# The upper column half of gates and projections with tokens stationary and 512 weight columns moving

## The chip, the cores and the metric

The kernel runs on one core of one Trainium2 chip. A time is device microseconds of one execution. The kernel before took 1406.93 us (median of three runs, 1406.03 to 1407.38). One execution was profiled; it took 1405.17 us, and its trace spans 1403.3 us.

## The reference

One block of a decoder, 256 tokens of width 2048, float32. In short:

```python
mod = silu(c) @ w_ada + b_ada                 # six vectors of 2048: sh1, sc1, g1, sh2, sc2, g2
h = rms_norm(x, norm_mix_g) * (1 + sc1) + sh1
u, q, k, v, ga, gb = split(h @ w_in)          # 1024 each, the two gates 2048 each
y_ssm = s5_branch(u, ...)                     # a scan over tokens, gelu, then y * sigmoid(y @ w_glu + b_glu)
y_att = moba_attention(q, k, v, rel_bias)     # 8 heads of 128, causal, with a bias by distance
merged = sigmoid(ga) * (y_ssm @ w_proj_ssm) + sigmoid(gb) * (y_att @ w_proj_attn)
x = x + g1 * (merged @ w_out)
h2 = rms_norm(x, norm_mlp_g) * (1 + sc2) + sh2
x = x + g2 * (square(relu(h2 @ w_ff1)) @ w_ff2)
return rms_norm(x, norm_final_g)
```

With 256 tokens there is one attention block, so attention is plain causal attention with a bias.

## The kernel before

**Arithmetic.** Every large product is made of three TensorE products in a shorter float format. Each operand is split into a high part, a copy by ScalarE (`split`, L144), and a low part, the difference, by VectorE (L146). A GEMM adds high x high, high x low and low x high in one PSUM bank.

**Weights.** All weights are streamed in tiles of 128 rows by 1024 columns (512 KB; `load`, L139, on SP's queue) into seven buffers `wraw`. ScalarE makes `whi`, VectorE `wlo`, with four buffers each, so the splits can be at most four steps ahead of TensorE. A *step* below is one such tile: its splits and its matmuls.

**Two forms of a GEMM.** In `gemm_t` (L172, matmuls L188 to L190) a 128x128 piece of the weights is stationary and the 256 tokens move; the result has output columns on the partitions. A step has 8 x 3 = 24 matmuls. In `gemm_n` (L297, L315 to L319) 128 tokens are stationary and 512 weight columns move; the result has tokens on the partitions. A step has 2 x 2 x 3 = 12 matmuls. Both fill four PSUM banks for 1024 columns; five banks are there for them (`bank`), three for the smaller work (`aux`), so of four banks of a new GEMM only the first is free before the last GEMM's banks are emptied.

**Stages.** Each stage of the table further down is a run of such GEMMs. First come eight column blocks of w_in (q, k, v, u and the lower half of gate ga) in parts, as the first modulation vectors become ready (`qkvu`). Then, with all 16 steps each: ga upper, gb lower, gb upper (the loop at L1138, i = 1, 2, 3). Then the projections with 8 steps each: `proj_attn(0)`, the GLU, `proj_attn(1)`, and the two halves of the SSM projection (L1187). Then w_out, the norm, and the MLP.

**What runs beside it.** *Lanes* are lists of small jobs; after each step every lane gains its rate and issues a job for each whole unit (`step`). The lane "ada" holds the products with w_ada that are not needed at once: each job loads 512 KB into a `wraw` buffer and VectorE multiplies and sums it (L374, 1.22 us). Its rate is set by stage: R2 and R3 in `qkvu`, RS0 to RS2 in the gates, RPA from the projections on, RWO in w_out. The lane "m" holds attention, head by head (scores `sco`, softmax on VectorE and ScalarE, transposes `ptr`, values `pav`), and from the middle of ga upper on the SSM branch in four parts (`ssm_in`: `vr` and `vi` on TensorE; `ssm_scan` on VectorE; `ssm_ys`: `ys`), then gelu and the way back to channel order.

**Order.** Within each engine instructions run in the order in which they stand. A scheduler sets that order when the program is built; it works from its own estimate of the times and from priorities (weight loads and splits stand ahead of their place in the code by `OFF`).

**Buffers that matter here.** Attention's scratch `asc` is six of the eight upper slices of ga (`ga[:, 8:14]`, L1110), two heads in turn. The gate's own result is copied there from PSUM by ScalarE (L1144) when attention has let go of the slices. `merged` is split into `mh` and `ml` in the buffer that held `ah` and `al`.

**Token order.** The SSM branch works on tokens in four interleaved phases (token = 4c + s). Before the change the GLU and the SSM projection keep the order (s, c), and the product with the gate reads and writes ga in permuted order (L1192).

Of the kernel before, what the change touches and what calls it, by code (L numbers as in the profile page):

```python
# [15 lines left out]
AF = mybir.ActivationFunctionType  # L16
# [3 lines left out]
P = 128  # L20
S = 256
# [25 lines left out]
SL = 6  # L47
R1 = 1.65
R2 = .95
R3 = .5  # L50
RS0 = .7
RS1 = .25
RS2 = .7
GR = (4, 6, 6)
RAT = 1.5
RSS = .43
RPA = .75
RWO = .5
RM = .55
NP = 4  # L60
# [13 lines left out]
class Kern:  # L74
# [219 lines left out]
            then.append((o, c))  # L294
        yield then

    def gemm_n(self, src, kts, c0, xh, xl, koff=0, tail=1, seeds=None):  # L297
        nc = self.nc
        banks = self.seeded("pn", seeds)
        n = len(kts)  # L300
        held, prev = [], None
        for i, unit in enumerate(self.stream(src, kts, c0)):
            u = (i,) + unit
            held.append(u)
            for t in range(2):
                if t and n - tail <= i < n - 1:
                    continue
                tk = slice(t * P, (t + 1) * P)
                for s in range(2):
                    o = banks[t * 2 + s]  # L310
                    c = slice(s * 512, (s + 1) * 512)
                    for q, kt, hi, lo in held if t else [u]:
                        kx = kt - koff
                        with self.after(prev if tail > 1 and i == n - 1 and t + s else None):
                            nc.tensor.matmul(o, xh[:, kx, tk], hi[:, c], start=q == 0 and not seeds, stop=False,  # L315
                                             skip_group_check=bool(seeds))
                            nc.tensor.matmul(o, xl[:, kx, tk], hi[:, c], start=False, stop=False,  # L317
                                             skip_group_check=bool(seeds))
                            self.mm = last = nc.tensor.matmul(o, xh[:, kx, tk], lo[:, c], start=False, stop=q == n - 1,  # L319
                                                              skip_group_check=bool(seeds))  # L320
                    prev = last
                if t:
                    held = []
        return banks
# [595 lines left out]
    def body(self):  # L920
# [217 lines left out]
        for i in range(1, 4):  # L1138
            if i == 3:
                self.lanes["ada"][1] = RS2  # L1140
            dst, c0 = ((ga, 4096), (ga, 5120), (gb, 6144), (gb, 7168))[i]
            banks = self.gemm_t(win, range(KT), c0, self.ah, self.al, mid=to_ssm if i == 1 else None)
            for b in range(4):
                nc.scalar.copy(dst[:, (i % 2) * 8 + 2 * b:(i % 2) * 8 + 2 * b + 2, :],  # L1144
                               banks[b].rearrange("p (k s) -> p k s", s=S))
# [11 lines left out]
        for k in range(4):  # L1157
            self.split(yh[:, 2 * k:2 * k + 2], yl[:, 2 * k:2 * k + 2], self.yatt[:, 2 * k:2 * k + 2])
        def proj_attn(cg):
            banks = self.gemm_t(a["w_proj_attn"][0], range(8), cg * 1024, yh, yl)  # L1160
            for b in range(4):
                d = gb[:, cg * 8 + 2 * b:cg * 8 + 2 * b + 2, :].rearrange("p k s -> p (k s)")
                v.tensor_mul(d, d, banks[b])
# [12 lines left out]
        for b in range(4):  # L1176
            t = sg[:, b]
            for k in range(2):
                nc.scalar.activation(t[:, k], banks[b][:, k * S:(k + 1) * S], AF.Sigmoid,
                                     bias=self.bglu[:, 2 * b + k:2 * b + k + 1])  # L1180
            s = slice(2 * b, 2 * b + 2)
            v.tensor_mul(sc4(t), sc4(t), yT[:, s])
            self.split(gg[:, 0, s], gg[:, 1, s], t)
        proj_attn(1)
        self.a2("mh")
        mh, ml = self.ah, self.al
        for cg in range(2):  # L1187
            banks = self.gemm_t(a["w_proj_ssm"][0], range(8), cg * 1024, gg[:, 0], gg[:, 1])
            for b in range(4):
                s = slice(cg * 8 + 2 * b, cg * 8 + 2 * b + 2)  # L1190
                d = ga[:, s, :]
                dk = d.rearrange("p k (c s) -> p k s c", s=4)  # L1192
                v.tensor_mul(dk, dk, banks[b].rearrange("p (k s c) -> p k s c", k=2, s=4))
                v.tensor_add(d, d, gb[:, s, :])
                self.split(mh[:, s], ml[:, s], d)
        self.lane("x", self.load_x(), .25, -.5)
        self.lane("g1", [lambda ch=ch: g1_row(ch) for ch in range(4)], .25)
        self.lanes["ada"][1] = RWO
# [261 lines left out]
```

## Time and profile before

| what | value |
|---|---|
| median of the runs | 1406.93 us |
| profiled execution | 1405.17 us, span 1403.3 us |
| TensorE busy | 98% of the span |
| VectorE busy | 74% |
| ScalarE busy | 53% |
| mean granted TensorE clock | 0.996 |

The stages that the prediction speaks of, in us from the span's start, by the first matmul of each:

| stage | form | steps | from | to |
|---|---|---|---|---|
| last third of the w_in blocks | both | 42 | 176.7 | 300.4 |
| ga upper | tokens moving | 16 | 300.4 | 360.6 |
| gb lower | tokens moving | 16 | 360.6 | 417.3 |
| gb upper | tokens moving | 16 | 417.3 | 471.9 |
| attention projection, first half; GLU | tokens moving | 8 + 8 | 471.9 | 518.4 |
| attention projection, second half | tokens moving | 8 | 518.4 | 541.5 |
| SSM projection, two halves | tokens moving | 8 + 8 | 541.5 | 589.7 |
| w_out, first half | weights moving | 16 | 589.7 | 634.4 |

A row of the view by stretches gives the stretch, its length, and for each engine the busy time and (x) the number of instructions, then the granted TensorE clock, the DMA engines' mean busy share and GB/s. A row of the view by groups gives source line, engine, operation, tiles (out<-in), shape and count, then busy time and mean ns of one, then the engine's idle time ahead of them and what ended it. A row of the timeline, or of the chain of waits, begins with start and length. PE is TensorE's matmuls, PEld its weight loads, DVE is VectorE, ACT is ScalarE. A matmul's recorded length includes its way through the array, so matmuls that follow each other overlap and their rate is read from their starts.

### The profile page before, as it was taken

To read this page: it belongs to the slowest core of one execution; us is meant where nothing else is said; L and a number is where in the kernel's file an instruction comes from. 1 tells how busy PE (TensorE), PEld (TensorE's weight loads), DVE (VectorE), ACT (ScalarE), POOL (GpSimd) and SP (SyncE) were. 2 spreads that over 40 slices of the span, in tenths; PEclk is the share of its full clock that TensorE was granted. 3 is DMA by queue.
4 is the path that set the end of the run, shared out by engine and by line. 5 is a ranking of instruction groups with operands and counts; after the bars stand their busy time and mean duration, and the time that the engine had idled before them with its cause. 6 is when DMAs were issued, how large, how long until landed. Compare 5 with 4: busy or idle time off the path is not lost.

```text
span 1403.3 us, 23470 instructions
## 1 busy us (share of the span) xinstructions
PE 1369.2 (98%) x9282; PEld 1219.2 (87%) x9282; DVE 1040.4 (74%) x1474; ACT 737.7 (53%) x1004; POOL 40.9 (3%) x94
## 2 busy tenths in 40 slices
PE   7889999999999999999999999999999999999997
PEld 5779899989999999988888888888888888888885
DVE  5788899776898888977777775777676555554676
ACT  4464565577545853446555554544463553635543
POOL 1000000410001300000000000000000000000000
PEclk9999999999999999999999999999999999999998
DMA  9999996885567988887588777778777566565551
GB/s 352 361 395 332 336 324 221 231 272 205 175 212 236 314 325 301 301 332 291 175 300 282 216 244 246 242 251 276 250 249 235 192 195 190 186 194 187 181 204 60
DMA packets 113293, 353.19 MB, mean 252 GB/s; under 512 B 12080, under 2 KB 12096, under 8 KB 113056
## 3 DMA queue, kind: packets, MB, share of 16 engines
q1 hardware_dynamic: 110096, 346.61, 72.1%
q0 software_dynamic: 2800, 4.58, 1.3%
q8 instruction: 72, 1.18, 0.3%
q10 hardware_dynamic: 288, 0.52, 0.1%
q14 instruction: 37, 0.30, 0.1%
HBM read 347.27 MB, written 2.29 MB: 249 GB/s over the span
## 4 chain that ended last, share of the span: by engine, by line
PE 86%; DMA 7%; DVE 4%; ACT 2%; issue 1%; DVEq 0%; SPq 0%; ACTq 0%
PE pw L216 15%; PE pn L315 9%; PE pn L317 9%; PE pn L319 9%; PE pt L188 8%; PE pt L190 8%; PE pt L189 8%; PE pw L218 8%; DMA wraw<-in_w_in_dram 5%; DVE wlo L146 2%; PE pn L246 2%; PE pn L247 2%; PE pn L248 2%; DVE wraw L374 1%; ACT whi L144 1%
## 5 line engine op out<-in xcount | busy, mean ns | idle before, releaser
L146 DVE TENSOR_TENSOR wlo<-wraw,whi 128x1024 fp32r<-128x1024 f32 x439 | 535.8, 1223 | 276.6 <-ACT whi L144 275.3
L144 ACT CAST whi<-wraw 128x1024 fp32r<-128x1024 f32 x439 | 460.5, 1051 | 531.7 <-PE pn L317 167.8
L216 PE MATMUL pw<-mh,whi 128*128 128x512 f32 x896 | 314.5, 397 | 0.0
L188 PE MATMUL pt<-ah,whi 128*128 128x256 f32 x896 | 251.9, 288 | 5.9 <-ACT whi L144 3.8
L189 PE MATMUL pt<-ah,whi 128*128 128x256 f32 x896 | 249.5, 284 | 0.0
L218 PE MATMUL pw<-mh,wlo 128*128 128x256 f32 x896 | 249.2, 281 | 0.0
L190 PE MATMUL pt<-ah,wlo 128*128 128x256 f32 x896 | 239.7, 286 | 1.4 <-DVE wlo L146 1.1
L374 DVE SCALAR_TENSOR_TENSOR wraw<-wraw,cb 128x1024 f32<-128x1024 f32 x176 | 213.5, 1219 | 0.0
L216 PEld LDWEIGHTS pw<-mh,whi 128*128 128x128 f32 x896 | 167.9, 188 | 39.5
L317 PE MATMUL pn<-whi,ff 128*128 128x512 f32 x480 | 187.0, 390 | 0.0
L315 PE MATMUL pn<-whi,ff 128*128 128x512 f32 x480 | 186.9, 389 | 0.0
L319 PE MATMUL pn<-wlo,ff 128*128 128x512 f32 x480 | 185.8, 389 | 0.0
L188 PEld LDWEIGHTS pt<-ah,whi 128*128 128x128 f32 x896 | 171.6, 192 | 10.3 <-ACT whi L144 5.4
L189 PEld LDWEIGHTS pt<-ah,whi 128*128 128x128 f32 x896 | 172.1, 192 | 0.4 <-DVE ah L146 0.2
L218 PEld LDWEIGHTS pw<-mh,wlo 128*128 128x128 f32 x896 | 169.1, 189 | 1.0
L190 PEld LDWEIGHTS pt<-ah,wlo 128*128 128x128 f32 x896 | 165.0, 192 | 3.8 <-DVE wlo L146 3.4
L315 PEld LDWEIGHTS pn<-whi,ff 128*128 128x128 f32 x480 | 90.1, 188 | 19.0
L319 PEld LDWEIGHTS pn<-wlo,ff 128*128 128x128 f32 x480 | 90.1, 188 | 18.7
L317 PEld LDWEIGHTS pn<-whi,ff 128*128 128x128 f32 x480 | 90.1, 188 | 18.5
L1354 DVE TENSOR_TENSOR y<-y,pn 128x512 f32<-128x512 f32 x48 | 31.0, 684 | 14.6 <-PE pn L319 14.6
L315 PE MATMUL pn<-whi,mh 128*128 128x512 f32 x96 | 37.7, 393 | 1.7 <-ACT whi L144 1.7
L317 PE MATMUL pn<-whi,mh 128*128 128x512 f32 x96 | 37.4, 389 | 0.0
(422 smaller groups left out, 1737.4 us busy)
## 6 DMA issues: line engine op xcount, KB each, us to landing
wraw<-in_w_ff_dram SPq DMA_DIRECT2D x256, 512.0 KB, 4.3
wraw<-in_wat_dram SPq DMA_DIRECT2D x176, 512.0 KB, 5.7
wraw<-in_w_in_dram SPq DMA_DIRECT2D x128, 512.0 KB, 5.5
wraw<-in_w_out_dram SPq DMA_DIRECT2D x32, 512.0 KB, 6.3
wraw<-in_wan_dram SPq DMA_DIRECT2D x16, 512.0 KB, 8.7
wraw<-in_w_proj_attn_dram SPq DMA_DIRECT2D x16, 512.0 KB, 6.5
wraw<-in_w_proj_ssm_dram SPq DMA_DIRECT2D x16, 512.0 KB, 6.7
wraw<-in_w_glu_dram SPq DMA_DIRECT2D x8, 512.0 KB, 5.7
```

Source lines behind the costliest of these rows:

```text
L144: h = self.nc.scalar.copy(hi, src)
L146: s = self.nc.vector.tensor_sub(lo, src, hi.bitcast(F32))
L188: nc.tensor.matmul(o, hi[:, c], xh[:, kx, :], start=st, stop=False, skip_group_check=True)
L189: nc.tensor.matmul(o, hi[:, c], xl[:, kx, :], start=False, stop=False, skip_group_check=True)
L190: self.mm = nc.tensor.matmul(o, lo[:, c], xh[:, kx, :], start=False, stop=sp, skip_group_check=True)
L216: nc.tensor.matmul(banks[b], hi[:, c], x2[:, k0 + k].rearrange("p h s -> p (h s)"), start=i + k == 0, stop=False, skip_group_check=True)
L218: self.mm = nc.tensor.matmul(banks[b][:, 0:S], lo[:, c], x2[:, k0 + k, 0, :], start=False, stop=i == n - 1 and k == 1, skip_group_check=True)
L315: nc.tensor.matmul(o, xh[:, kx, tk], hi[:, c], start=q == 0 and not seeds, stop=False, skip_group_check=bool(seeds))
L317: nc.tensor.matmul(o, xl[:, kx, tk], hi[:, c], start=False, stop=False, skip_group_check=bool(seeds))
L319: self.mm = last = nc.tensor.matmul(o, xh[:, kx, tk], lo[:, c], start=False, stop=q == n - 1, skip_group_check=bool(seeds))
L374: v.scalar_tensor_tensor(w, w, 1.0, self.cb[:, (i % 2) * 1024:(i % 2 + 1) * 1024], op0=OP.mult, op1=OP.mult, accum_out=pc[:, i:i + 1])
L1354: v.tensor_add(d, d, banks[b])
```

## The change

The upper 1024 columns of both gates, of the attention projection and of the SSM projection are computed by `gemm_n` instead of `gemm_t`: 16 + 16 + 8 + 8 steps. Their results, the gate products and the sum then have tokens on the partitions. The merged rows of that half are brought back by 16 transposes on TensorE (four for each PSUM bank) and split from PSUM. The GLU's sigmoid writes its result in natural token order, and what follows (its product with y, the SSM projection, the merge) uses that order, so that the product with ga is no longer permuted. `gemm_n` gets a call-back in its middle, which ga upper needs. The rate of the ada lane goes from .5 to .8 in the last part of `qkvu` (R3) and from .75 to .55 in the projections (RPA).

```diff
-R3 = .5
+R3 = .8
...
-RPA = .75
+RPA = .55
...
-    def gemm_n(self, src, kts, c0, xh, xl, koff=0, tail=1, seeds=None):
+    def gemm_n(self, src, kts, c0, xh, xl, koff=0, tail=1, seeds=None, mid=None):
...
+            if mid and i == n // 2:
+                mid()
...
-            banks = self.gemm_t(win, range(KT), c0, self.ah, self.al, mid=to_ssm if i == 1 else None)
+            gemm = self.gemm_n if i % 2 else self.gemm_t
+            banks = gemm(win, range(KT), c0, self.ah, self.al, mid=to_ssm if i == 1 else None)
...
-            banks = self.gemm_t(a["w_proj_attn"][0], range(8), cg * 1024, yh, yl)
+            banks = (self.gemm_n if cg else self.gemm_t)(a["w_proj_attn"][0], range(8), cg * 1024, yh, yl)
...
-                nc.scalar.activation(t[:, k], banks[b][:, k * S:(k + 1) * S], AF.Sigmoid,
+                nc.scalar.activation(t[:, k].rearrange("p (c s) -> p s c", s=4),
+                                     banks[b][:, k * S:(k + 1) * S].rearrange("p (s c) -> p s c", s=4), AF.Sigmoid,
                                      bias=self.bglu[:, 2 * b + k:2 * b + k + 1])
             s = slice(2 * b, 2 * b + 2)
-            v.tensor_mul(sc4(t), sc4(t), yT[:, s])
+            v.tensor_mul(t.rearrange("p k (c s) -> p k c s", s=4), t.rearrange("p k (c s) -> p k c s", s=4),
+                         self.yT.rearrange("p s k c -> p k c s")[:, s])
...
-            banks = self.gemm_t(a["w_proj_ssm"][0], range(8), cg * 1024, gg[:, 0], gg[:, 1])
+            banks = (self.gemm_n if cg else self.gemm_t)(a["w_proj_ssm"][0], range(8), cg * 1024, gg[:, 0], gg[:, 1])
...
-                dk = d.rearrange("p k (c s) -> p k s c", s=4)
-                v.tensor_mul(dk, dk, banks[b].rearrange("p (k s c) -> p k s c", k=2, s=4))
+                v.tensor_mul(d, d, banks[b].rearrange("p (k s) -> p k s", k=2))
                 v.tensor_add(d, d, gb[:, s, :])
-                self.split(mh[:, s], ml[:, s], d)
+                if cg == 0:
+                    self.split(mh[:, s], ml[:, s], d)
+                    continue
+                p = self.aux("trm")
+                flat = d.rearrange("p k s -> p (k s)")
+                for k in range(4):
+                    nc.tensor.transpose(p[:, k * P:(k + 1) * P], flat[:, k * P:(k + 1) * P], self.ident)
+                ks, tk = slice(8 + 4 * (b % 2), 12 + 4 * (b % 2)), slice(b // 2 * P, (b // 2 + 1) * P)
+                self.split(mh[:, ks, tk], ml[:, ks, tk], p.rearrange("p (k s) -> p k s", s=P))
```

The scheduler lays the work out anew. Three places matter. (In the change all lines stand two or three further down.)

On TensorE, the end of ga upper. Before, the last head's value product and the first SSM input block stand within the last step of ga upper (`pt_3426` to `pt_3429` are its banks):

```order
L188 MATMUL pt_3427<-ah,whi 128x256
L781 MATMUL pav<-ga,v 128x256
L782 MATMUL pav<-ga,v 128x128
L864 MATMUL vr<-u_3045,bp 64x64 x16
L864 MATMUL vi<-u_3045,bp 64x64 x16
L189 MATMUL pt_3427<-ah,whi 128x256
```

Now, in gb lower (`pt_4012` to `pt_4015`), where the third bank is first used:

```order
L188 MATMUL pt_4013<-ah,whi 128x256
L189 MATMUL pt_4013<-ah,whi 128x256
L190 MATMUL pt_4013<-ah,wlo 128x256
L783 MATMUL pav<-ga,v 128x256
L784 MATMUL pav<-ga,v 128x128
L775 MATMUL ptr<-ident,ga 128x128 x3
L188 MATMUL pt_4014<-ah,whi 128x256
L189 MATMUL pt_4014<-ah,whi 128x256
```

This value product is the seventh head's and the transposes are the eighth's. The value products of three heads (the sixth to the eighth) and the first SSM input block have moved from ga upper into the first steps of gb lower, and the first two banks of gb lower go through four steps before its third begins.

On VectorE, the late steps of gb lower, where the splits of the weights and the SSM scans alternate. Now, between the splits of steps 14 and 15 (`rw`, `sri`, `tbl` are the SSM branch's tiles; sixteen such operations stand here, these are the first and the last):

```order
L146 TENSOR_TENSOR wlo<-wraw,whi 128x1024
L873 TENSOR_TENSOR rw<-rw 128x512
L874 TENSOR_TENSOR rw<-vi,tbl 128x512
L883 SCALAR_TENSOR_TENSOR rw<-rw 128x512
...
L892 TENSOR_TENSOR sri<-sri,rw 128x8x63
L871 TENSOR_TENSOR rw<-vr,tbl 128x512
L872 TENSOR_TENSOR rw<-vi,tbl 128x512
L146 TENSOR_TENSOR wlo<-wraw,whi 128x1024
```

Before, the longest such block in this stage is eight operations. The SSM branch's second part starts later and catches up here.

On TensorE, the first half of w_out. Now, 41 matmuls after its start (`pn_6475` to `pn_6478` are its banks):

```order
L321 MATMUL pn_6477<-wlo,mh 128x512
L317 MATMUL pn_6478<-whi,mh 128x512
L319 MATMUL pn_6478<-whi,mh 128x512
L321 MATMUL pn_6478<-wlo,mh 128x512
L321 MATMUL pn_6475<-wlo,mh 128x512
L1205 MATMUL trm<-ident,ga 128x128 x12
L321 MATMUL pn_6476<-wlo,mh 128x512
```

Twelve of the sixteen new transposes stand there together, the other four some three steps later; before, there is nothing but matmuls of w_out and a few small transposes for g1 in this place.

## The prediction

> **What bounds the kernel now.** I read the page first, then the busy times by stage, then single instructions in order of time.
>
> ```profile
> span 1403.3 us, 23470 instructions
> PE 1369.2 (98%) x9282; PEld 1219.2 (87%) x9282; DVE 1040.4 (74%) x1474; ACT 737.7 (53%) x1004; POOL 40.9 (3%) x94
> PE 86%; DMA 7%; DVE 4%; ACT 2%; issue 1%; DVEq 0%; SPq 0%; ACTq 0%
> ```
>
> TensorE is busy for 98% of the span and holds 86% of the chain of waits. An average hides stages, so the next view cuts the stretch that is edited. In order: the last third of the first GEMM phase; gates ga upper, gb lower, gb upper; attention projection (first half) with the GLU; its second half; the two halves of the SSM projection; the first half of w_out.
>
> ```profile
> core 0: us, PE busy (x) PEld busy (x) DVE busy (x) ACT busy (x) POOL busy (x), PEclk, DMA share, GB/s
> 176.70:300.40 123.70, 123.38 (x1317) 117.91 (x1317) 105.33 (x144) 74.17 (x112) 19.67 (x40) 1.00 0.79 254
> 300.40:360.60 60.20, 60.19 (x526) 58.79 (x525) 41.24 (x75) 41.28 (x82) 0.00 (x0) 1.00 0.67 235
> 360.60:417.30 56.70, 56.70 (x707) 55.90 (x705) 54.95 (x72) 28.78 (x35) 0.00 (x0) 1.00 0.57 183
> 417.30:471.90 54.60, 54.60 (x642) 54.00 (x641) 47.21 (x68) 31.38 (x39) 15.26 (x32) 1.00 0.77 253
> 471.90:518.40 46.50, 46.50 (x390) 46.50 (x389) 38.69 (x53) 27.64 (x34) 0.07 (x1) 1.00 0.90 324
> 518.40:541.50 23.10, 23.10 (x195) 23.10 (x194) 20.86 (x32) 12.24 (x18) 0.00 (x0) 1.00 0.91 315
> 541.50:564.50 23.00, 23.00 (x194) 23.00 (x194) 19.13 (x25) 8.39 (x8) 0.00 (x0) 1.00 0.90 327
> 564.50:589.70 25.20, 23.50 (x194) 23.21 (x193) 24.40 (x33) 10.38 (x12) 0.00 (x0) 1.00 0.78 269
> 589.70:634.40 44.70, 44.70 (x206) 37.09 (x205) 37.34 (x48) 20.65 (x23) 0.00 (x0) 1.00 0.89 342
> ```
>
> Everywhere but in the last SSM projection (1.7 us of TensorE idle) PE equals the window, at clock 1.00. So what shortens the PE queue in these stages shortens the span, as long as VectorE keeps up: it stands at 97% in the gb lower gate and in the last SSM projection.
>
> **The main term: matmul pitch.** A busy PE is not a PE at its peak, so I take the starts. First a stretch with weights stationary and 256 tokens moving, then one of the first w_out half, with tokens stationary and 512 columns moving:
>
> ```profile
> 544.82 0.28 PE L189 MATMUL pt<-gg,whi 128*128 128x256 f32 x1
> ...
> 546.25 0.28 PE L190 MATMUL pt<-gg,wlo 128*128 128x256 f32 x1
> ```
> ```profile
> 619.68 0.39 PE L317 MATMUL pn<-whi,mh 128*128 128x512 f32 x1
> ...
> 622.18 0.39 PE L315 MATMUL pn<-whi,mh 128*128 128x512 f32 x1
> ```
>
> The first pair lies 12 matmuls apart: 1.43/12 = 0.119 us. The SSM projection's first half agrees: 8 steps of 24 matmuls in 23.00 us are 0.120. The second pair lies 11 apart: 2.50/11 = 0.227 us. A step over 128 rows of the weights costs 24 x 0.120 = 2.88 us the old way and 12 x 0.227 = 2.72 us the new way. The four edited GEMMs have 16 + 16 + 8 + 8 = 48 steps, so this is 48 x 0.156 = **-7.5 us** (by 0.119 it would be -6.4, by the exact 23.00/192 and 2.50/11 -7.1; with 0.226 -8.1: -6.4 to -8.1).
>
> In the Trainium skill, "TensorE: Matmul & The Clock Gate", section "Back-to-back issue gap", a warm matmul alone costs N/2.4 + 2.5 ns: 109 and 216 ns. By it, as an estimate, two narrow matmuls against a wide one save 2.5 ns, 1.4 us over the 576 pairs. The trace does not agree: 2 x 0.120 - 0.227 leaves 13 ns a pair.
>
> **Transposes of the merged rows.** 16 new TensorE transposes, 128x128, are the same operation as these:
>
> ```profile
> 820.99 1.47 PE L1296 MATMUL trf<-ident,part 128*128 128x128 f32 x12
> L1296 PE MATMUL trf<-ident,part 128*128 128x128 f32 x16 | 2.1, 272 | 0.0
> ```
>
> (1.47 - 0.27)/11 = 0.109 us each, so 16 x 0.109 = **+1.75 us**. They stand on PE within w_out, where PE is the bound: nothing hides them. They are issued 41 matmuls (9.3 us) after w_out begins, and VectorE's four products and four sums before them need 8 x 0.69 = 5.5 us, so they should not be waited for. The upper half of the merged rows is first needed at step 8, 21.8 us in.
>
> **VectorE in the projections.** Two rows of the stretch from the ga upper gate to w_out, the product read in permuted order and the one read straight, then the two standing costs of a step, from the page:
>
> ```profile
> L1193 DVE TENSOR_TENSOR ga<-ga,pt 128x512 f32<-128x512 f32 x8 | 8.7, 1106 | 0.0
> L1163 DVE TENSOR_TENSOR gb<-gb,pt 128x512 f32<-128x512 f32 x8 | 5.1, 681 | 0.0
> ```
> ```profile
> L146 DVE TENSOR_TENSOR wlo<-wraw,whi 128x1024 fp32r<-128x1024 f32 x439 | 535.8, 1223 | 276.6 <-ACT whi L144 275.3
> L374 DVE SCALAR_TENSOR_TENSOR wraw<-wraw,cb 128x1024 f32<-128x1024 f32 x176 | 213.5, 1219 | 0.0
> ```
>
> Eight products go from 1.106 to 0.68 us (-3.4 us of VectorE), and the lower w_ada rate takes 8 sums of 1.22 us out of the projections (30 to 22 in VectorE's queue). The GLU's four products and eight sigmoids now stride; were they all 1.1 us it would be +1.7 on VectorE, behind the 21.8 us of the projection that follows. So VectorE has 103.1 - 3.4 - 9.8 + 1.7 = 91.6 us of work in the four projection windows, of 115.3, instead of 103.1 of 117.8. Does that remove the one stall?
>
> ```profile
> 577.09 6.31 DMA wraw<-in_w_out_dram
> 583.50 1.05 ACT whi L144
> 584.60 0.50 PE pn L315
> ```
>
> The first w_out tile is asked for at 577.1, when VectorE at last frees a buffer, and PE waits for its ScalarE copy until 584.6. The window's 25.2 us less 8 x 2.88 are 2.2, of which two early w_out matmuls take 0.2. All 2.0 may go (-2.0); or VectorE's block of sums and splits after the first SSM half stays as late and PE only arrives 8 x 0.156 = 1.25 us earlier (+1.25). In the new order that block is undivided (eight operations, 5.5 us) but with one w_ada sum ahead of it instead of several. I take half of the gain: **-1.0 us**.
>
> **Gate stage: attention now ends later.** Attention's scratch lies in the upper half of ga, so three of the ga upper gate's four banks can't be emptied before the last heads are through. In the new order three heads have moved behind that GEMM, and PE meanwhile takes two banks of the gb lower gate through four steps. From the fifth head's value product to the eighth's PE has 76 narrow and 7 wide matmuls and 4.2 us of attention: 9.1 + 1.6 + 4.2 = 14.9 us. Before it had
>
> ```profile
> 338.11 0.43 PE pav L781 x2
> 338.54 0.22 PE pav L782 x2
> 338.76 0.22 PE sco L754 x2
> 338.98 0.43 PE sco L755 x2
> 345.37 0.43 PE pav L781 x2
> 350.36 0.43 PE pav L781 x2
> 356.24 0.43 PE pav L781 x2
> 356.89 1.08 PE vr L864 x32
> 357.97 0.93 PE vi L864 x32
> ```
>
> 18.1 us from 338.1 to 356.2 (a value product is 0.65 us, a score 0.65, a head's three transposes 3 x 0.109; 3, 2 and 3 of them make the 4.2). That was PE's spacing, not attention's need: head 8's weights were scaled by 350.4 and PE took them at 352.6.
>
> ```profile
> 349.91 0.49 ACT L766 ACTIVATE ga<-ga,ast 128x256 f32<-128x256 f32 x1
> ```
> ```profile
> 352.64 0.27 PE L773 MATMUL ptr<-ident,ga 128*128 128x128 f32 x1
> ```
>
> So the cost lies between 0 and 18.1 - 14.9 = 3.2 us; with 2.2 us to spare per head I put it near the lower end. The SSM work slides too: some ten VectorE operations of 0.68 us move from the ga upper gate to the gb lower one, 54.95 + 6.9 = 61.8 us of VectorE against 56.7 + 5.3 = 62.0 of PE (three value products, a score, two heads' transposes and the SSM input block's 2.0 move along): even. I take a fifth of attention's bound, **+0.7 us**.
>
> **w_ada rates.** Nine sums of 1.22 us enter the first window above: 105.3 + 11.0 = 116.3 of 123.7 us. Its first part is tight,
>
> ```profile
> 176.70:233.80 57.10, 56.78 (x562) 55.98 (x561) 54.75 (x72) 35.23 (x50) 0.00 (x0) 1.00 0.85 291
> ```
>
> and with three sums there 58.4 of 57.1: 0 to +1.3 us, if the weights' lead (four buffers) does not cover it. It should: **+0.3 us**.
>
> **Sum.** -7.5 + 1.75 - 1.0 + 0.7 + 0.3 = -5.75 us. The profiled execution took 1405.17 us; that gives 1399.4. The median of the runs lies 1.76 higher, so I forecast **1401.2 us**. The terms' ends give -8.1 + 1.75 - 2.0 = -8.35 (1398.6) and -6.4 + 1.75 + 1.25 + 3.2 + 1.3 = +1.1 (1408.0).
>
> **Rivals.**
> 1. *The gain is eaten* (0.17). Attention keeps its old pace (+3.2 instead of 0) and the first w_out tile stays late (+1.25 instead of -1.0): -5.75 + 3.2 + 2.25 = -0.3, 1406.6 us. For it: VectorE at 97% in two of the stages. Against: the spare 2.2 us, and 11.5 us less VectorE work in the projections.
> 2. *Slower* (0.11): attention's lateness pushes the SSM scans into one block. VectorE's new queue holds 16 SSM operations between the splits of steps 14 and 15 of the gb lower gate and 7 more before the next stage's first: 23 x 0.68 + 2 x 1.22 = 18.1 us, against 4 x 2.88 = 11.5 us of PE in the four steps that the buffers hold. If VectorE begins that block when PE has no SSM work of its own left, PE stands 6.6 us, beside attention's 3.2: -5.75 + 3.2 + 6.6 = +4.05, 1411.0 us. Against it: an SSM input and an SSM output block on PE stand between those steps (the gb upper window's 54.6 - 16 x 2.88 = 8.5 us hold one input block of 2.0 and two output blocks, so 5.2 together), so it decides only from a VectorE queue several us late. For it: 54.95 busy of 56.70.
> 3. *Width saves nothing here* (0.04): a wide matmul in these stages costs two narrow ones, 0.240. Then +1.75 - 1.0 + 0.7 + 0.3 = +1.75, 1408.7 us. Against it: 0.227 in w_out, where the stationary tile sits in the same buffer as the gates' `ah`. By the Trainium skill's figure above, 1.4 us would come off that, 1407.3 us.
>
> The forecast has 0.66 and its own range is 1398.6 to 1403.5; 0.02 is left. A measurement of this kernel tells about 0.2% (2.8 us) from no change. Faster than that: 0.66 plus a few hundredths of rival 1, 0.69; within it: 0.19; slower: 0.12. The range that holds the time 8 times in 10: **1397.8 to 1407.5**.
>
> **What would show it.** Pitch: wide matmuls 0.227 us apart in the ga upper gate and the three others; the attention projection's second half at 8 x 2.72 = 21.8 us instead of 23.1, the gb upper gate near 52.1. Transposes: 16 at 0.11 us in w_out, with no wait for VectorE. Attention: no TensorE gap at the first bank change of the gb lower gate; a gap until a ScalarE copy of ga is rival 1, one until `wlo` near its end is rival 2. The prediction is wrong if the edited GEMMs are not shorter, or if the stages behind w_out change length.

## The result, and the profile after

The changed kernel took 1414.06 us (median of seven runs, 1410.31 to 1418.47), the kernel before 1404.77 us (seven runs, 1402.88 to 1407.38). The ratio is 1.0066, with a 95% interval of 1.0053 to 1.0079: slower by 9.3 us, where I forecast faster by 5.7. The predicted 1401.2 us and its range (1397.8 to 1407.5) both missed. The medians of runs 1 and 13 further down leave out three single executions that took 2605 us or more, as a disturbed execution says nothing of the kernel.

First the page of the changed kernel: span, busy times, and the shares of the chain of waits by engine.

```profile
span 1411.9 us, 22353 instructions
PE 1367.8 (97%) x8722; PEld 1192.2 (84%) x8722; DVE 1038.5 (74%) x1474; ACT 737.0 (52%) x1004; POOL 40.8 (3%) x94
PE 79%; DMA 8%; DVE 7%; ACT 3%; issue 2%; DVEq 0%; SPq 0%; ACTq 0%
```

TensorE has less to do (1367.8 us against 1369.2), but its share of the chain falls from 86% to 79%: the new time is waiting. The view by stretches of the changed kernel, cut at the same stages as before (from the last third of the first GEMM phase to the first half of w_out; columns as in the prediction), says where:

```profile
176.50:304.70 128.20, 123.64 (x1314) 118.33 (x1313) 111.24 (x158) 69.57 (x101) 19.67 (x40) 0.99 0.84 277
304.70:357.80 53.10, 52.86 (x251) 43.53 (x250) 39.41 (x68) 39.04 (x78) 0.00 (x0) 1.00 0.79 272
357.80:421.30 63.50, 62.58 (x791) 61.00 (x789) 52.79 (x75) 33.26 (x52) 0.00 (x0) 1.00 0.46 146
421.30:477.70 56.40, 54.23 (x452) 45.04 (x449) 51.12 (x73) 29.15 (x38) 14.79 (x32) 0.97 0.74 246
477.70:526.70 49.00, 47.08 (x385) 46.26 (x384) 37.24 (x47) 29.95 (x37) 0.46 (x1) 1.00 0.90 314
526.70:548.50 21.80, 21.80 (x98) 18.06 (x97) 20.24 (x26) 12.43 (x17) 0.00 (x0) 1.00 0.75 262
548.50:571.60 23.10, 23.10 (x194) 23.08 (x193) 18.53 (x25) 8.39 (x8) 0.00 (x0) 1.00 0.91 322
571.60:593.30 21.70, 21.70 (x97) 17.98 (x97) 18.66 (x26) 9.52 (x11) 0.00 (x0) 1.00 0.65 213
593.30:642.30 49.00, 47.80 (x226) 39.12 (x225) 38.56 (x51) 21.61 (x25) 0.00 (x0) 1.00 0.91 341
```

Set against the same rows of before, by stage (us; each stage ends at the first matmul of the next; the part ahead of these rows agrees with before to 0.2, the part behind them is 0.7 longer):

| stage | before | changed | difference | predicted |
|---|---|---|---|---|
| last third of the w_in blocks | 123.7 | 128.2 | +4.5 | +0.3 |
| ga upper, gb lower, gb upper | 171.5 | 173.0 | +1.5 | -5.0 + 0.7 = -4.3 |
| attention projection, first half; GLU | 46.5 | 49.0 | +2.5 | 0 |
| attention projection, second half | 23.1 | 21.8 | -1.3 | -1.25 |
| SSM projection | 48.2 | 44.8 | -3.4 | -1.25 - 1.0 |
| first half of w_out | 44.7 | 49.0 | +4.3 | +1.75 |
| sum | 457.7 | 465.8 | +8.1 | -5.75 |

The two projection rows came as predicted or better. Four places lost. The view of TensorE's waits of the changed kernel, over the end of the first phase, then over the gates and the attention projection, then over w_out (engine, line, what it waited for: us in total, times, longest):

```profile
PE pn L317 <- ACT whi L144: 3.3, 1, 3.3
```
```profile
PE ys L904 <- DVE sri L892: 2.2, 1, 2.2
PE pt L188 <- ACT whi L144: 1.6, 1, 1.6
PE vi L866 <- issue: 0.8, 1, 0.8
PE pt L190 <- DVE wlo L146: 0.3, 1, 0.3
```
```profile
PE pn L317 <- ACT whi L144: 0.8, 1, 0.8
PE pn L321 <- DVE wlo L146: 0.4, 1, 0.4
```

**End of the first phase.** The wait of 3.3 us is in the last block (v), where before has none. It begins at VectorE. The sixteen operations that build the SSM branch's table `rt` (by which `ys` is made from `u`), first in the kernel before, then in the changed kernel:

```profile
255.08 1.92 DVE L704 SCALAR_TENSOR_TENSOR rt<-rk,rmask,rt 128x512 f32<-128x512 f32 x3 [1.07 <-PE rk L698]
257.14 1.23 DVE L146 TENSOR_TENSOR wlo<-wraw,whi 128x1024 fp32r<-128x1024 f32 x1
258.28 2.56 DVE L704 SCALAR_TENSOR_TENSOR rt<-rk,rmask,rt 128x128 f32<-128x128 f32 x5
262.83 1.23 DVE L146 TENSOR_TENSOR wlo<-wraw,whi 128x1024 fp32r<-128x1024 f32 x1 [1.99 <-ACT whi L144]
...
265.12 4.01 DVE L704 SCALAR_TENSOR_TENSOR rt<-rk,rmask,rt 128x512 f32<-128x512 f32 x8
```
```profile
263.23 9.07 DVE L706 SCALAR_TENSOR_TENSOR rt<-rk,rmask,rt 128x512 f32<-128x512 f32 x16 [2.09 <-PE rk L700]
```

Before, they stand in three pieces with weight splits between; now they are one block. SP's queue, which issues the weight requests, waits for VectorE's splits to free a buffer (250 to 300 us, before and then changed: us in total, times, longest):

```profile
SPq L139 <- DVE wlo L146: 30.6, 10, 5.7
```
```profile
SPq L139 <- DVE wlo L146: 17.4, 4, 11.9
```

The chain of waits of the changed kernel just behind the block, and then the stretches around it:

```profile
273.35 1.23 DVE wraw L376 x2
274.57 1.14 DVE wlo L146
275.71 1.16 DVE wraw L376 x2
276.88 13.14 DMA wraw<-in_w_in_dram
```
```profile
264.00:272.00 8.00, 7.15 (x181) 6.95 (x178) 7.58 (x15) 2.67 (x5) 6.22 (x14) 1.00 0.56 170
272.00:280.00 8.00, 8.00 (x69) 8.00 (x68) 7.13 (x10) 1.82 (x2) 5.41 (x11) 1.00 0.95 167
280.00:288.00 8.00, 4.65 (x24) 3.57 (x24) 2.45 (x3) 3.35 (x5) 3.32 (x7) 0.91 1.02 211
288.00:296.00 8.00, 8.00 (x35) 6.73 (x34) 4.01 (x9) 4.16 (x7) 0.07 (x1) 0.88 1.03 355
```

From 263.2 to 272.3 VectorE does nothing but `rt` (8.6 us of work). No weight split gets through, no `wraw` buffer comes free, SP issues nothing between 261.16 and 273.45, and the DMA engines fall to 56%. Then VectorE alternates splits and w_ada sums, and six requests for 512 KB tiles go out within 6 us. The one that matters, the fourth, goes out at 276.88 and takes 13.14 us to land, where the page gives 5.6 as the median for these tiles. The DMA engines are full then (0.95, 1.02) but move 167 to 211 GB/s, against 355 a little later: small transfers of the bias table (`tz`) and of the SSM input (`u`), issued by POOL, run beside the tiles. DMA issues of the changed kernel from 262 to 288 us, then of the kernel before from 259 to 285 us (transfer, queue, count, size, median us from issue to landing):

```profile
wraw<-in_w_in_dram SPq DMA_DIRECT2D x4, 512.0 KB, 12.1
tz<-scr POOLq DMA_DIRECT2D x8, 128.0 KB, 7.0
u<-uT POOLq DMA_DIRECT2D x24, 32.0 KB, 5.3
```
```profile
wraw<-in_w_in_dram SPq DMA_DIRECT2D x6, 512.0 KB, 5.5
tz<-scr POOLq DMA_DIRECT2D x8, 128.0 KB, 5.9
u<-uT POOLq DMA_DIRECT2D x28, 32.0 KB, 4.9
```

So the small transfers alone don't make the landing slow: before has as many of them (POOL's queue takes 35% of the DMA engines' time in both windows), and its tiles land in 5.5 us. What differs is the silence of 12 us and the bunch behind it: three other tiles are under way when the request of 276.88 goes out. How much of the 13.14 us is the bunch and how much the small transfers beside it isn't shown; no run moved either alone.

### The profile page after: what moved, and what is told of

Same layout as the page of the kernel before. It is cut to its first block, busy times and chain, and to the rows that moved or that the text cites. A ratio compares the mean times of both kernels' runs of the same rounds, so it can differ in the third digit from the quotient of the medians.

```text
span 1411.9 us, 22353 instructions
## 1 busy us (share of the span) xinstructions
PE 1367.8 (97%) x8722; PEld 1192.2 (84%) x8722; DVE 1038.5 (74%) x1474; ACT 737.0 (52%) x1004; POOL 40.8 (3%) x94
## 4 chain that ended last, share of the span: by engine, by line
PE 79%; DMA 8%; DVE 7%; ACT 3%; issue 2%; DVEq 0%; SPq 0%; ACTq 0%
PE pw L216 15%; PE pn L317 11%; PE pn L319 11%; PE pn L321 11%; PE pw L218 7%; DMA wraw<-in_w_in_dram 6%; PE pt L188 5%; PE pt L189 5%; PE pt L190 5%; DVE wlo L146 3%; DVE wraw L376 2%; PE pn L246 2%; PE pn L247 2%; PE pn L248 1%; ACT whi L144 1%
## 5 line engine op out<-in xcount | busy, mean ns | idle before, releaser
L188 PE MATMUL pt<-ah,whi 128*128 128x256 f32 x640 | 176.9, 287 | 6.3 <-ACT whi L144 4.0
L189 PE MATMUL pt<-ah,whi 128*128 128x256 f32 x640 | 176.6, 285 | 0.0
L190 PE MATMUL pt<-ah,wlo 128*128 128x256 f32 x640 | 163.8, 286 | 1.0 <-DVE wlo L146 0.8
L188 PEld LDWEIGHTS pt<-ah,whi 128*128 128x128 f32 x640 | 122.4, 192 | 9.3 <-ACT whi L144 5.1
L189 PEld LDWEIGHTS pt<-ah,whi 128*128 128x128 f32 x640 | 123.2, 193 | 0.5 <-DVE ah L146 0.2
L190 PEld LDWEIGHTS pt<-ah,wlo 128*128 128x128 f32 x640 | 115.1, 193 | 2.9 <-DVE wlo L146 2.6
L317 PE MATMUL pn<-whi,ah 128*128 128x512 f32 x192 | 76.6, 400 | 8.7 <-ACT whi L144 8.4
L319 PE MATMUL pn<-whi,ah 128*128 128x512 f32 x192 | 75.2, 392 | 0.0
L321 PE MATMUL pn<-wlo,ah 128*128 128x512 f32 x192 | 68.0, 395 | 0.1
```

Of the source, the lines that this page charges most:

```text
L188: nc.tensor.matmul(o, hi[:, c], xh[:, kx, :], start=st, stop=False, skip_group_check=True)
L189: nc.tensor.matmul(o, hi[:, c], xl[:, kx, :], start=False, stop=False, skip_group_check=True)
L190: self.mm = nc.tensor.matmul(o, lo[:, c], xh[:, kx, :], start=False, stop=sp, skip_group_check=True)
```

## The experiments

Every run was timed in turn with the kernel before on the same chip; the chips differ between groups of runs (medians of the kernel before: 1404.9, 1405.4, 1404.6 and 1405.7 us for runs 1 to 4, 5 to 8, 9 to 11 and 12 to 14). Stage lengths are from one profile of each. Ratios are to the kernel before and are the numbers to compare across groups.

### Rates or form: runs 1 to 4

Run 1, the changed kernel with one number put back:

```diff
-R3 = .8
+R3 = .5
```

> The change with R3 back at .5 (RPA stays .55). Theory A (rates): the nine w_ada sums that R3 = .8 adds hold weight buffers while VectorE is busy with the SSM tables, so TensorE starves late in the w_in blocks (3.8 us in one gap at 286.8 us of the changed profile, the stage's end 5.1 us later than before) and attention and the SSM branch start late behind it. It expects the gap gone and 1400 to 1406 us, 8 to 14 us under the change. Theory B (form): the wide form of the gates makes attention and the SSM branch late by itself (scheduling, banks). It expects the 5 us of the w_in blocks back at most and 1408 to 1412 us, with the waits in gb lower, gb upper and the first attention projection still there.

Measured: 1403.8 us, ratio 0.9994 (0.9985 to 1.0003). One number is worth 10 us. The wait at the end of the first phase is gone, and the block of that stage has its old 18.1 us.

Run 2, both rates put back:

```diff
-R3 = .8
+R3 = .5
-RPA = .55
+RPA = .75
```

> The change with both rates as before (R3 .5, RPA .75): the form and the token order alone. Theory A: 1400 to 1406 us; against the run with R3 alone back it loses up to 2 us, as the projections carry eight more w_ada sums on VectorE. Theory B: 1408 to 1414 us.

Measured: 1412.22 us, ratio 1.0054 (1.0040 to 1.0067). With R3 good, the old RPA costs the new form 8.4 us (run 2 less run 1); the first half of the SSM projection takes 30.1 us instead of 23.0. TensorE's waits there, and stretches of 2 us around them (that from 543 to 545 left out):

```profile
PE pt L188 <- ACT whi L144: 2.7, 2, 1.6
PE pt L190 <- DVE wlo L146: 0.8, 1, 0.8
```
```profile
541.00:543.00 2.00, 0.50 (x2) 0.30 (x2) 0.79 (x3) 1.04 (x1) 0.00 (x0) 1.00 1.03 412
545.00:547.00 2.00, 1.26 (x6) 1.26 (x7) 2.00 (x5) 0.69 (x1) 0.00 (x0) 0.50 1.06 401
547.00:549.00 2.00, 2.00 (x11) 2.00 (x11) 1.15 (x2) 0.00 (x0) 0.00 (x0) 0.50 0.80 301
549.00:551.00 2.00, 2.00 (x13) 2.00 (x13) 0.00 (x0) 0.00 (x0) 0.00 (x0) 0.61 0.84 250
```

Three short gaps, some 4 us in all, stand within 5.5 us; the DMA engines are full at 401 to 412 GB/s. From 543.8, behind the second of them, the granted clock is 0.50 until 550.6: 11 matmuls in 2 us instead of 17. The gaps make 4 us of the 7, the clock the other 3.

Run 3, the kernel before with the two new rates and nothing else:

```diff
-R3 = .5
+R3 = .8
-RPA = .75
+RPA = .55
```

> The kernel before with the two new rates alone. Theory A: the last w_in blocks end some 5 us later, the stall ahead of w_out (2 us) goes, and the time is 1406 to 1410 us, slower than before. Theory B: the rates are harmless in the old form, 1401 to 1405 us.

Measured: 1410.13 us, ratio 1.0037 (1.0022 to 1.0052): the rates alone make the old form 5 us slower. The last block of the first phase takes 23.5 us instead of 18.1, with the same wait, while the stall ahead of w_out is gone (the SSM projection's second half takes 23.0 us). So theory A holds for R3. The gates take 172.8 us here, as in the changed kernel (173.0): at R3 = 0.8 the wide form gains nothing in them by these two profiles.

Run 4, the rates put back and the gates in the old form:

```diff
-R3 = .8
+R3 = .5
-RPA = .55
+RPA = .75
-            gemm = self.gemm_n if i % 2 else self.gemm_t
+            gemm = self.gemm_t
```

> The change with the rates as before and the two upper gate halves in the narrow form again; the projections stay wide and the transposes stay. The gates then pair with projection results of another layout, so the upper half of the merged rows is not the reference's; the amount of work is the same. Theory B: gate stages as before (60, 57 and 55 us), the projections 2.5 us shorter, transposes 1.75 us: 1402 to 1405 us, and clearly under the run with both rates back. Theory A: 5 us slower than the run with both rates back (32 steps at 0.156 us), which has nothing wrong in its gates.

Measured: 1412.48 us, ratio 1.0057 (1.0039 to 1.0074), as run 2. The gates' form changes nothing here, and the loss is the same stall in the SSM projection (30.5 us).

### What the projections' rate and the transposes cost: runs 5 to 8

Run 5, the kernel before with one rate:

```diff
-RPA = .75
+RPA = .55
```

> The kernel before with one number changed: the w_ada rate in the four projections from 0.75 to 0.55 (the gate rate stays at 0.5, all GEMMs as before). Theory A (the rate matters through the first w_out tile, which waits for a buffer that the sums hold: in the run with both rates alone this stall of 2.0 us is gone): about -2.0 us, 1402.9. Theory B (the sums that leave the projections cost the same time where they go, in the first half of w_out): no change, 1404.9, with w_out's first half about 2 us longer.

Measured: 1404.22 us, ratio 0.9988 (0.9978 to 0.9997). In the profile 2.2 us leave the SSM projection's second half, but its whole span is no shorter (1403.9; this execution, at 1406.81 us, was the longest of the twelve): waits of 1.3 and 0.5 us for weights turn up behind w_out's first half. The stall goes as theory A says; at least part of it is paid later, and the medians show 1.2 us left of the gain.

Run 6, run 1 with the gates in the old form:

```diff
-            gemm = self.gemm_n if i % 2 else self.gemm_t
+            gemm = self.gemm_t
```

> The changed kernel with the gate rate back at 0.5, the projection rate left at 0.55, and both gates in the old narrow form (so only the projections are wide; layouts are then mixed, and the merged values are not the reference's). It is to be compared with the run that differs from it in the gates' form alone, 1403.9. Theory A (the wide gates give back in VectorE waits of the SSM blocks and at the attention projection's first tiles what 32 steps at 0.156 us, 5.0 us, save): 1403.9 within 1.5, the gate stages at their old lengths of 60.2, 56.6 and 54.6 us. Theory B (the wide gates keep most of their gain): 1407 to 1409.

Measured: 1403.29 us, ratio 0.9986 (0.9975 to 0.9996), beside 1403.8 us and 0.9994 for run 1, which ran on another chip. Theory A: at R3 = 0.5 the wide gates save nothing. Their stages are 60.1, 56.6 and 54.6 us here; in run 1 they are 54.5, 61.2 and 54.6, and 1.9 us more are lost at the attention projection's first tiles. TensorE's longest waits of run 1 in the gates and the start of the attention projection:

```profile
PE ys L904 <- DVE sri L892: 1.7, 1, 1.7
PE pt L190 <- DVE wlo L146: 0.8, 1, 0.8
```

From 300 to 472 us before has no wait in this view.

Run 7, run 1 with a lower rate in w_out:

```diff
-RWO = .5
+RWO = .35
```

> The changed kernel with the gate rate back at 0.5 and the w_ada rate in w_out lowered from 0.5 to 0.35. Theory A (w_out's first half is 4.5 us longer than before: 1.75 of it transposes, and some 2 us waits for weight tiles whose buffers the w_ada sums hold): the waits go, the first half of w_out comes to about 47.3 us, and the time to about 1402, unless later stages take the tiles badly. Theory B (the waits come from the merge's own VectorE block of products, sums and splits, not from w_ada): w_out's first half stays at 49.2 and the time at 1403.9.

Measured: 1410.71 us, ratio 1.0035 (1.0024 to 1.0046). Theory B for w_out: its first half takes 48.7 us, that of run 1 48.6 (up to the first matmul of the second half; the 49.2 and 47.3 of the expectation reach 0.5 us further). The sums that were put off cost more later, where one wait of 4.8 us in the MLP's first GEMM appears.

Run 8, run 1 without the transposes:

```diff
-                if cg == 0:
-                    self.split(mh[:, s], ml[:, s], d)
-                    continue
-                p = self.aux("trm")
...
-                self.split(mh[:, ks, tk], ml[:, ks, tk], p.rearrange("p (k s) -> p k s", s=P))
+                self.split(mh[:, s], ml[:, s], d)
```

> The changed kernel with the gate rate back at 0.5 and without the 16 transposes of the merged rows: the upper half is split as it lies (so what w_out multiplies is not the reference's). Theory A (the transposes cost their own 1.7 us on TensorE and nothing else): w_out's first half 47.5 us, time 1402.2. Theory B (the splits behind the transposes wait for them, and so hold back the VectorE queue and the buffers of w_out's tiles): the 2 us of waits in w_out's first half go too, about 45.5 us there, time 1400.

Measured: 1400.68 us, ratio 0.9968 (0.9956 to 0.9980): 3.1 us less than run 1 (3.7 by the ratios, on two chips), some twice the transposes' own time. That time was predicted well; the group of them in the changed kernel and, from its timeline, twelve together:

```profile
L1205 PE MATMUL trm<-ident,ga 128*128 128x128 f32 x16 | 2.1, 272 | 0.0
604.42 1.47 PE L1205 MATMUL trm<-ident,ga 128*128 128x128 f32 x12
```

By starts all sixteen hold the queue for 1.68 us. The first half of w_out takes 43.9 us in run 8 and 48.6 in run 1. Of these 4.7 us some 1.2 are no gain: run 8's order has most of the small transposes for g1 in the projections, which take 1.4 us more there without any gap, and run 1's has them in w_out. Another 1.5 us are gaps at the first w_out tiles in run 1, which run 8 doesn't have. Theory B's number is the nearer one, but how the splits behind the transposes would hold back a tile was not isolated, and run 12 below has the transposes without these gaps.

### Attention's place, and R3 between: runs 9 to 14

Run 9, run 1 with attention issued faster:

```diff
-RAT = 1.5
+RAT = 2.0
```

> The changed kernel with the gate rate back at 0.5 and attention issued faster (rate of its lane from 1.5 to 2.0): in the queue the last head's value product moves from three steps into gb lower to one and a half, and the first SSM block with it. Theory A (the wide gates' gain is eaten because attention, and behind it the SSM scans, come late: an SSM output waits 2.3 us for VectorE in gb upper, and the attention projection's first tiles 1.9 us): half of these waits go, about -2 us, 1402. Theory B (these waits come from VectorE's total work in the two gb gates, which the order doesn't change): 1403.9 within 1.

Measured: 1402.82 us, ratio 0.9985 (0.9976 to 0.9994); run 1 had 0.9994 (0.9985 to 1.0003), so the two can hardly be told apart. In the profile gb upper falls from 54.6 to 52.8 us, as theory A says, but the wait at the attention projection grows from 1.9 to 3.0.

Run 10, the SSM lane too:

```diff
-RAT = 1.5
+RAT = 2.0
-RSS = .43
+RSS = .5
```

> As the run with the faster attention, and the SSM's lane from 0.43 to 0.5 as well: the last SSM output stands at step 4 of gb upper in the queue instead of step 9. Theory A (late SSM scans eat the gates' gain): the wait of an SSM output in gb upper and the wait at the attention projection's first tiles (4.2 us together) go, 1400 to 1401. Theory B (VectorE's total work in the gates): the waits move into gb lower, where VectorE then has more to do, and the time is 1404 to 1407.

Measured: 1403.23 us, ratio 0.9987 (0.9978 to 0.9995). The two waits of theory A go: gb upper 50.7 us, the attention projection's first half 23.0. But gb lower grows from 61.2 to 65.1, as theory B says. Nothing measurable is won.

Run 11, the changed kernel with R3 halfway:

```diff
-R3 = .8
+R3 = .65
```

> The changed kernel with the gate rate R3 at 0.65, halfway between the 0.5 that gave 1403.9 and the 0.8 that gave 1414.1. Theory A (the extra sums cost in proportion, each delaying the weight tiles by VectorE's time): about 1409, and a wait of some 2.5 us in the last block of the first phase. Theory B (a threshold: the four split weights in hand cover a few sums, and a wait begins only when VectorE's block of SSM table work falls behind a run of them): 1404 with no wait there, or 1414 with the whole of it.

Measured: 1403.98 us, ratio 1.0000 (0.9990 to 1.0010). Neither theory had this. The wait in the last block is there in full (the block takes 24.3 us), which speaks for a threshold; yet the total is 10 us better than at 0.8, because the gates with the attention projection's first half now take 190.2 us, 4.3 less than before (194.5). That is the gain that I had predicted for the gates. As with 0.8, `rt` is one block of sixteen operations, and SP's longest wait for a split is 13.7 us.

Runs 12 and 13, just below the threshold that the built queues show: with 0.55 and 0.6 the products `rk`, which feed the `rt` operations, stand two blocks ahead of the last one of the first phase, as they do with 0.5; with 0.65 and 0.8 they stand in the block before it. (The two expectations call this the bias table; it is the SSM branch's table.)

```diff
-R3 = .8
+R3 = .55
```

> The changed kernel with the gate rate R3 at 0.55 instead of 0.8. In the queue the products of the bias table (rk) then stand two blocks ahead of the last block of the first phase, as with 0.5, and not in the block before it, as with 0.65 and 0.8; and attention ends at 1.6 steps of gb lower, as with 0.65. Theory A (two separate costs: the wait in the last block comes when the bias table's VectorE work slides next to it, whatever the number of sums; the gates' gain comes when attention ends early): no wait in the last block (18.1 us, not 23 to 24), gates to the attention projection's first half 4 us shorter than before, together 1398 to 1400. Theory B (the shorter gates of the run at 0.65 were a gift of that wait, which let weights and w_ada run ahead): no wait, but gates as long as before, 1403 to 1404.

```diff
-R3 = .8
+R3 = .6
```

> The same with R3 at 0.6, the highest of the built rates at which the bias table's products still stand two blocks ahead. Theory A (position in the queue decides): as at 0.55, 1398 to 1400, no wait in the last block. Theory C (the number of sums decides: twice as many more than at 0.55): a wait there of some 3 us, and 1401 to 1403.

Measured: 1401.44 us, ratio 0.9971 (0.9959 to 0.9983), and 1402.9 us, ratio 0.9974 (0.9963 to 0.9985). In both the last block takes 18.1 us, with no wait in the view. The sums grow from 0.5 to 0.65 step by step and the wait comes all at once, where the order of `rt` changes: in run 12 it stands as 8 and 8 operations, in run 13 as 7 and 9, with a split between, and SP's longest wait for a split is 6.8 us in both. So the order decides, as far as these runs go; none moved `rt` at the same number of sums. Run 12 is faster than both kernels, by 0.3% against the kernel before. Its three gates and the attention projection's first half with the GLU, by stretches:

```profile
300.00:353.70 53.70, 53.70 (x260) 44.91 (x259) 38.01 (x70) 38.42 (x77) 0.00 (x0) 1.00 0.74 248
353.70:414.50 60.80, 60.80 (x781) 59.50 (x779) 55.90 (x74) 31.39 (x40) 0.00 (x0) 1.00 0.56 179
414.50:466.70 52.20, 52.20 (x451) 43.57 (x449) 47.60 (x69) 28.43 (x36) 14.88 (x32) 1.00 0.78 248
466.70:514.50 47.80, 47.05 (x386) 46.36 (x385) 37.53 (x47) 30.36 (x37) 0.48 (x1) 1.00 0.92 319
```

PE equals the window in the first three. The gates take 166.7 us, 4.8 less than before; gb upper's 52.2 is the 52.1 of the prediction. The attention projection's first tiles are 1.7 us late, 0.8 of it a wait for `wlo` that the profile shows.

So of the two theories for run 12, A has the mechanism (the wait and the gates' gain come apart), while the time lies between the two forecasts, 1.4 us above A's upper end. Run 13's 1402.9 us lies where theory C had it, but without C's wait.

Run 14, the kernel before with both rates at 0.55:

```diff
-R3 = .5
+R3 = .55
-RPA = .75
+RPA = .55
```

> The kernel before, its GEMMs as they were, with both w_ada rates at 0.55: what the rates alone give, beside the same rates with the wide form. Theory A (the wide form is worth what the prediction counted without its R3 term and without the stall that the rate removes, 7.5 less 1.75 less 0.7, so 5 us, once the rates suit it): 1403 to 1404 here, against 1398 to 1400. Theory B (the rates alone do it): within 1 us of the wide form's time.

Measured: 1403.35 us, ratio 0.9980 (0.9969 to 0.9991). That is theory A's number, but the distance to the wide form isn't the 5 us that it counts. The form is worth 1.9 us beside run 12 by the medians, but the two intervals overlap, so the time alone does not show that it is worth anything. The stages of one profile of each do: run 12's take 3.2 us less from the gates to w_out's first half (us):

| stage | old form (run 14) | wide (run 12) | difference | predicted for the form |
|---|---|---|---|---|
| three gate GEMMs | 171.0 | 166.7 | -4.3 | -4.3 |
| attention projection, first half; GLU | 46.0 | 47.8 | +1.8 | 0 |
| attention projection, second half | 23.1 | 21.8 | -1.3 | -1.25 |
| SSM projection | 46.1 | 44.8 | -1.3 | -1.25 |
| first half of w_out | 45.3 | 47.2 | +1.9 | +1.75 |
| sum | 331.5 | 328.3 | -3.2 | -5.05 |

## Why the prediction was wrong, by its own steps

**Main term, pitch: right.** The attention projection's second half took 21.8 us and the SSM projection's 21.7, eight steps of 2.72. The third rival (width saves nothing) is out. By the figure of the Trainium skill that I weighed (page "TensorE: Matmul & The Clock Gate", section "Back-to-back issue gap") these two would have saved nearly nothing; they saved 1.3 us each.

**Transposes: their own time right** (1.68 us for 1.75); they were not waited for, as the trace's idle time of 0.0 ahead of them shows. In run 12 they cost w_out what was priced (1.9 us against run 14, with no wait). In the changed kernel gaps of 1.7 us at the first w_out tiles come on top (next paragraph); their cause stays open.

**VectorE in the projections: half right.** The product durations came as priced, the straight ones shorter and the GLU's at the 1.1 us that I had put as their bound; two rows of the changed kernel's groups:

```profile
L1186 DVE TENSOR_TENSOR sg<-sg,yT 128x512 f32<-128x512 f32 x4 | 4.3, 1108 | 0.0
L1197 DVE TENSOR_TENSOR ga<-ga,pn 128x512 f32<-128x512 f32 x4 | 2.5, 682 | 0.0
```

The lower RPA did remove the stall at the end of the SSM projection (2.0 us of gaps to 0.0). But 1.7 us of gaps now stand among w_out's first tiles, so the term was about 0 and not -1.0. With the old rate it would have been far worse, 7 us (run 2), and in another place, the SSM projection's first half; in the range its bad end was +1.25. I had priced that end as a late arrival only, without TensorE's own slow clock behind the gaps.

**w_ada rates, R3: the step that failed first.** I counted VectorE's load over stretches, found the tight one at 176.7 to 233.8, and bounded the cost at +1.3 us because "the weights' lead (four buffers)" should cover it. The loss stands at 281 to 290, and is +4.5 us. The share of busy time was no measure of it. With the extra sums the scheduler laid all of `rk` together and one block later, so that `rt`, three pieces before, became 8.6 us of VectorE in one piece. Behind it SP's queue waited 11.9 us for a buffer, where its longest wait before is 5.7. The requests then came in a bunch, beside the small transfers, and TensorE stood. Run 3 shows this wait without the wide form, runs 12 and 13 show it gone with higher rates than before. The front of this document showed three places in the queues, and this was not one of them: I read R3 as a number of sums and not as a new order.

**Gate stage: the mechanism was named, its size and place were off.** I took +0.7 for late attention and gave 0.11 to rival 2, in which the SSM scans come late behind it. Attention itself cost TensorE next to nothing: its value products from the fifth head to the eighth lie 15.4 us apart (14.9 counted), and at the first bank change of gb lower no gap is over 0.3 us. Rival 2's time, 1411.0 us, is the nearest of the four to the 1414.06 measured, and that is luck. (Rivals 1 and 2 add attention's 3.2 to a sum that still holds its 0.7; with it counted once they are 1405.9 and 1410.3.) Its place was not the one that came: not a wait of 6.6 us for `wlo` late in gb lower, but an SSM output waiting for VectorE's last `sri` in gb upper, a wait at `vi` in gb lower, and weight tiles at the attention projection. VectorE's work in gb lower, counted as 61.8 us, was 52.8 of 63.5; the scans slid on into gb upper (51.1 of 56.4). In the table the gates are 5.8 us worse than the term, and the attention projection's first half with the GLU 2.5. The SSM outputs of gb upper hold TensorE 9.8 us where before has 5.9 (by starts); of these 3.9 us only 2.2 are the wait itself. The rest is clock, in the stretches around it:

```profile
448.00:456.00 8.00, 5.83 (x58) 4.84 (x58) 6.17 (x11) 4.78 (x8) 0.00 (x0) 0.86 0.98 373
456.00:464.00 8.00, 8.00 (x84) 6.95 (x82) 6.40 (x10) 5.58 (x9) 4.73 (x10) 0.92 0.65 204
```

That this belongs to the order that R3 brings, and not to the wide form by itself, is shown by runs 11 to 13, with 52.2 to 52.6 us for the same gb upper. At R3 = 0.5 (run 1) it is there in part, with attention three steps into gb lower as at 0.8; at 0.55 to 0.65 attention ends one and a half steps earlier. Run 10 shows that an earlier place alone is not enough, since VectorE then lacks the time in gb lower.

**The sum.** With the rates that suit it, the form gives -3.2 in the stages where -5.05 was counted. The difference, 1.9, is the late weight tiles at the attention projection (1.8); the other rows came within 0.2. What stays open: why exactly those first tiles are late by 1.7 to 3.0 us in most wide versions (runs 1, 8, 9, 12, 13) and not in runs 10 and 11. In part the wait only changes its place: runs 1, 2, 7 and 8 have the same rates up to there and take 195.2 to 195.5 us for the gates with the attention projection's first half, but in runs 2 and 7 its tiles are only 0.3 to 0.4 us late and gb upper is 1.2 to 1.9 us longer than in run 1.

## What to carry to other kernels

A number that sets the rate of a side stream is an edit of the order: build the queues for it and look for long undivided blocks of the splitting engine (here 8.6 us of VectorE) in front of a place where weight requests must go out, rather than at busy shares. Scan such a number in small steps (0.5, 0.55, 0.6, 0.65 and 0.8 gave 0.9994, 0.9971, 0.9974, 1.0000 and 1.0066 of the time before) before judging the larger change that came with it. And price a TensorE gap of a few us above its length when the clock falls behind it: here 2.4 us cost 3.9, 3.6 cost 5.0, 4.5 (run 11) cost 6.2, and run 2's 4.1 cost 7.1.

## What the runs showed of the hardware

**Gaps of about 2 us can halve TensorE's clock.** In run 2 gaps of 1.86 and 1.04 us (between starts) within 3.2 us were followed by 0.214 us between narrow matmuls instead of 0.12, from 543.8 until 550.6. A single gap can do it: in the changed kernel one of 2.38 us at 451.5 was followed by a granted clock of 0.50 from 453.8 to 457.2, in run 2 one of 1.96 us at 445.5 by 0.50 from 448.2 to 451.6. Not every one does: before has one of 1.98 us at 582.6 and run 1 one of 2.10 at 444.1, and the clock stays at 1.00. The Trainium skill, "TensorE: Matmul & The Clock Gate", section "What's actually happening", has the array at half clock after an idle window of about 3.4 us and back at full after as long a busy one. The half agrees (0.50 granted), and so does the 3.4 us at half clock behind the single gaps; run 2's other stretch lasted 6.8. None of these gaps is 3.4 us long, so in this trace shorter ones do it.

**Full DMA engines, half the bytes.** At the end of the first phase the same share of DMA time (1.02 to 1.03) carried 211 GB/s with the small transfers under way and 355 when few of them were left. The 512 KB weight tile asked for at 276.88, with three others and the small transfers under way, took 13.14 us.
